# A hybrid decoder layer on one core: TensorE in written order from z through the attention, memory keys and values from one pass over rows of weights, token-major x loaded in halves and again later

## The chip, the core and the metric

The kernel runs on one core of a Trainium2 chip. The metric is device time of one execution, in microseconds (us). Before the change it is 1020.95 us, the median of 3 runs (1020.81 to 1021.11).

## What is computed

One decoder layer on 256 tokens of width 2048, in fp32 (cut to what matters here; SEQ = MEM_LEN = 256):

```python
h = rms_norm(x, g_mix)
z_pool, z_q, z_kv, z_kr, z_mq = split(h @ w_in)          # 512 | 512 | 256 | 64 | 512 columns
y_pool = pool_mixer(z_pool, w_pool, pool_scale)
y_mla  = mla_mixer(z_q, z_kv, z_kr, ...)                 # 8 causal heads, 128 + 64 wide, values 128
y_mem  = memory_cross_attention(z_mq, mem, ...)          # 4 heads of 128
x = x + concat(y_pool, y_mla, y_mem) @ w_o
x = x + conv_glu_ffn(rms_norm(x, g_ffn), ...)            # D_FF = 5632
# memory_cross_attention:
mkv = rms_norm(mem, g_mem) @ w_mem_kv                    # 2048 x 1024: keys 512 | values 512
k = rms_norm(keys per head) ; p = softmax(q k^T / sqrt(128)) ; o = p v
```

## The kernel before

Every large product is made of three fp32r products: weights and activations are each split into a high part (ScalarE copy to fp32r) and a low part (VectorE: value minus high part), and TensorE adds high x high, low x high and high x low. `split_w` (L92) splits 1024 columns of weights at a time into tiles `wh` and `wl`, three buffers each; `load_w` (L82) brings the weights through SyncE's queue into three `wr` buffers. `gemm_t` (L103) gives outputs with features on partitions: per 8 blocks of k, 8 matmuls of 512 columns (L116, `wh`) and 8 of 256 columns (`wl`). `gemm_n` (L121) gives outputs with tokens on partitions: per block of k, token half and output bank three matmuls of the same width (L132, L133, L134). PSUM is two pools of four banks, `psm` and `psa`.

The stages up to the attention, in the order of the program:

- Memory (L283 to L308): `mem_kv(0)` computes the keys in four chunks of 1 MB weights (four blocks of k each), and casts the memory rows `mg` from `memT` on the way (`mem_parts`, L248); `mem_kv(1)` goes over k again for the values, loads the transposed x (`xT_d`, 2 x 1 MB, SyncE's queue), casts it to `xg` (`x_parts`, L259) and finishes the keys (`mem_keys`, L268: scale, head norms, transposes). Sums of squares of the memory go through `SumSq.add` (L200).
- x in token-major form, `x1n` (2 x 1 MB, GpSimd's queue, L336), is loaded once; ScalarE squares it (L341), and later the output projection adds to it.
- mq and rope key (L355 to L375): 16 blocks of k in gemm_n with 288-column matmuls, then row norms and transposes (`to_features`, L226).
- Memory attention: `mem_attn(h)` for 4 heads (L416, L424). `softmax_pv` (L387) does a head's row maxima, exponentials and division, transposes of the weights p (L406), the copy `pT` (L409), the products with the values (L411, L412) and the split of the result (L414).
- z (L437 to L450): six gemm_t of 32 matmuls; then the latent scales (L453 to L462), whose column sums (L217) go over the squares of z.
- The up-projections and the pool branch (L571 to L592), then rope keys (L593 to L604).
- Attention (L633 to L639): `mla(h)` for 8 heads (scores L611 to L614, then `softmax_pv`), and after each head half of one column block of the output projection (`out_part`, L617: 24 matmuls of 512 columns). `out_part(1, ...)` (L662) adds the part over the heads' outputs.

The matmuls of the scores, transposes and values are plain fp32 (a 128- or 256-column product is two instructions; a transpose is one); all others of the list are fp32r. The order on each engine is made by a list scheduler from program order, dependences and its own estimate of times; `keep` (L88) pins an instruction behind the one that was traced before it on its engine. Before the change only a few instructions in this part are kept (L341, L345).

Of the kernel before, what the change touches and what calls it, by code (L numbers as in the profile page):

```python
# [11 lines left out]
F32 = mybir.dt.float32  # L12
# [48 lines left out]
def layer(ctx, tc, xT_d, xn_d, memT_d, vec_d, tab_d, w_z_d, w_mqkr_d, w_q_d, w_kv_d, w_mem_d, w_pool_d, w_o_d,  # L61
# [41 lines left out]
    def gemm_t(ps, raw, o, act, ks, first=True, last=True):  # L103


        ks = list(ks)
        nk = HS // P
        cs = range(0, len(ks), nk)
        for c in cs:
            kc = ks[c:c + nk]  # L110
            hi, lo = split_w(raw, o + c * P, len(kc) * P)

            for low in ((False, True) if c // nk % 2 == 0 else (True, False)):
                for i, k in enumerate(kc):
                    w = (lo if low else hi)[:, i * P:(i + 1) * P]
                    nc.tensor.matmul(ps[:, T if low else 0:2 * T], w, act(k)[:, 0:T] if low else act(k),  # L116
                                     start=first and c + i == 0 and not low,
                                     stop=last and c == cs[-1] and i == len(kc) - 1 and low == (c // nk % 2 == 0),
                                     skip_group_check=True)

    def gemm_n(pss, hi, lo, act, k0, first, last):  # L121
# [4 lines left out]
        for i in range(nk):  # L126
            for tt in range(NT):
                xh = act[:, k0 + i, tt * P:(tt + 1) * P]
                xl = act[:, k0 + i, T + tt * P:T + (tt + 1) * P]
                for j in range(nj):  # L130
                    ps, o = pss[tt][j], slice(j * w, (j + 1) * w)
                    nc.tensor.matmul(ps, xh, hi[:, i, o], start=first and i == 0, stop=False)  # L132
                    nc.tensor.matmul(ps, xl, hi[:, i, o], start=False, stop=False)  # L133
                    nc.tensor.matmul(ps, xh, lo[:, i, o], start=False, stop=last and i == nk - 1)  # L134

    def split_act(dst, src, scale=None):
# [4 lines left out]
        else:  # L141
            nc.scalar.activation(dst[:, 0:T], src, AF.Copy, scale=scale)
            nc.vector.scalar_tensor_tensor(dst[:, T:2 * T], src, scale, dst[:, 0:T].bitcast(F32),
                                           op0=ALU.mult, op1=ALU.subtract)
# [48 lines left out]
    class SumSq:  # L193
# [6 lines left out]
        def add(self, ch):  # L200
            sq = s4()
            nc.scalar.activation(sq[:], ch, AF.Square)
            if self.first:
                nc.vector.tensor_tensor(self.acc[:], sq[:, 0:2, :], sq[:, 2:4, :], op=ALU.add)
            else:
                for h in (0, 2):
                    nc.vector.tensor_tensor(self.acc[:], self.acc[:], sq[:, h:h + 2, :], op=ALU.add)
# [18 lines left out]
    def to_features(dst, src, tt, n, scale=None, eng=None):  # L226

        ps = ps_aux()
# [15 lines left out]
    for a, b in ((0, 1), (1, 2), (2, 4)):  # L244
        nc.sync.dma_start(raw0[:, a * 512:b * 512], w_mem_d[0][:, a * 512:b * 512])
        nc.sync.dma_start(xT[:, a:b, :], memT_d[:, a:b, :])

    def mem_parts(a, b):  # L248
        for j in range(a, b):
            split_act(mg[:, j, :], xT[:, j, :], v("g_mem", j))  # L250
# [8 lines left out]
    def x_parts(a, b):  # L259
        for j in range(a, b):  # L260
            split_act(xg[:, j, :], xT[:, j, :], v("g_mix", j))

    pss_k = []
# [4 lines left out]
    def mem_keys():  # L268
        ps = ps_aux()
        col_sums(ps, ms.done())  # L270
        rsqrt_(rm, ps[:, 0:2], 1.0 / D)
        for tt in range(NT):
            p3 = pss_k[tt][0].rearrange("p (h d) -> p h d", d=XD)
            t = tok()
            t3 = t[:].rearrange("p (h d) -> p h d", d=XD)
            f = fmk[:, tt * XH:(tt + 1) * XH]
            nc.scalar.activation(t3, p3, AF.Copy, scale=rm[:, tt:tt + 1])
            head_sq(f, t3)
            rsqrt_(f, f, 1.0 / XD)
            nc.vector.tensor_tensor(t3, t3, f.unsqueeze(2).to_broadcast([P, XH, XD]), op=ALU.mult)  # L280
            to_features(mkT, t, tt, XH, None, "v")

    def mem_kv(n):  # L283
        pss = [[ps_main()[:]] for _ in range(NT)]
        if n == 0:
            pss_k.extend(pss)
        for c in range(4):
            raw = raw0 if n + c == 0 else load_w(w_mem_d[n * 4 + c], STG, HS if n == 0 else STG)
            if n == 1 and c < 2:
                h = slice(c * 8, c * 8 + 8)  # L290
                nc.sync.dma_start(xT[:, h, :], xT_d[:, h, :])
            if n == 1 and c == 2:
                mem_keys()
            if n == 0 and c < 3:
                nc.sync.dma_start(xT[:, c * 4 + 4:c * 4 + 8, :], memT_d[:, c * 4 + 4:c * 4 + 8, :])
            for i in range(2):
                if n == 0:
                    mem_parts(c * 4 + i * 2, c * 4 + i * 2 + 2)
                elif c > 1:
                    x_parts((c - 2) * 8 + i * 4, (c - 2) * 8 + i * 4 + 4)  # L300
                hi, lo = split_w(raw, i * HS, HS, 512 if n + c == 0 else HS)
                gemm_n(pss, hi[:].rearrange("p (k n) -> p k n", n=512), lo[:].rearrange("p (k n) -> p k n", n=512),
                       mg, c * 4 + i * 2, c + i == 0, c == 3 and i == 1)
            if n == 0:
                ms.add(xT[:, c * 4:(c + 1) * 4, :])
        return pss

    mem_kv(0)  # L308
# [5 lines left out]
    nc.vector.tensor_tensor(gqk[:, 0:1], v("gq_nope"), v("gk_nope"), op=ALU.mult)  # L314
# [625 lines left out]
```

## Time and profile before

| | |
|---|---|
| median of 3 runs | 1020.95 us |
| the profiled execution | 1021.14 us, of which 1019.1 us is the span from first to last instruction |
| TensorE busy | 1013.6 us, 99% |
| VectorE, ScalarE, GpSimd busy | 752.6, 578.8 and 15.3 us |
| granted TensorE clock, mean | 0.999 |
| moved by DMA | 198.06 MB |

Busy time of TensorE is the union of its matmuls, whose ends overlap the next ones' beginnings; what one matmul costs is therefore read from the distance between two starts, not from its duration.

### The profile page before, as it was taken

The page shows a single profiled execution, that of the slowest core. Times are in us where ns is not written, and L with a number is a line of the kernel's source. Part 1 is how long each engine was busy: PE and PEld are TensorE (multiplying, and loading weights), DVE is VectorE, ACT ScalarE, POOL GpSimd, SP SyncE. Part 2 cuts the span into 40 slices and gives each one's busy share as a digit, 9 for nine tenths or more (in the row PEclk, how much of TensorE's full clock was granted, in tenths as well). Part 3 has the DMA queues.
Part 4 walks back from the last instruction along what each step waited for, and adds up shares of the span by engine and source line. Part 5 has one row for each costly group of instructions (what it writes and reads, how often), then busy time and mean ns, then how long its engine had stood idle before and what let it go on. Part 6 is the DMA issues. An engine that isn't in the chain of part 4 may idle for free.

```text
span 1019.1 us, 14119 instructions
## 1 busy us (share of the span) xinstructions
PE 1013.6 (99%) x5356; PEld 867.2 (85%) x5356; DVE 752.6 (74%) x1134; ACT 578.8 (57%) x853; POOL 15.3 (2%) x33
## 2 busy tenths in 40 slices
PE   9999999999999999999999999999999999999998
PEld 7898888877888888888888888888888888888886
DVE  7947689756677777777777776777676788888886
ACT  7657666554566555555555555555555555545653
POOL 0000000000000000000000000000000000010000
PEclk9999999999999999999999999999999999999999
DMA  9765444333665555545455555545555665575551
GB/s 349 289 204 185 160 168 168 132 125 124 226 214 183 205 178 194 192 181 205 167 207 182 190 194 180 205 168 205 186 187 199 256 212 202 206 286 210 206 207 42
DMA packets 30611, 198.06 MB, mean 194 GB/s; under 512 B 3536, under 2 KB 4048, under 8 KB 8656
## 3 DMA queue, kind: packets, MB, share of 16 engines
q1 hardware_dynamic: 28368, 189.44, 52.1%
q0 software_dynamic: 1888, 7.34, 2.0%
q8 instruction: 42, 0.69, 0.3%
q10 hardware_dynamic: 288, 0.38, 0.1%
q14 instruction: 25, 0.20, 0.1%
HBM read 192.96 MB, written 4.19 MB: 193 GB/s over the span
## 4 chain that ended last, share of the span: by engine, by line
PE 98%; DMA 1%; ACT 0%; DVE 0%; SPq 0%; issue 0%
PE psm L116 54%; PE psm L134 6%; PE psm L132 6%; PE psm L133 6%; PE psm L770 4%; PE psa L770 4%; PE psm L768 4%; PE psa L769 4%; PE psa L768 4%; PE psm L769 4%; PE psa L230 1%; PE psa L411 1%; PE psa L406 1%; DMA wr<-in_w_mem 1%; PE psa L611 1%; PE psa L612 1%
## 5 line engine op out<-in xcount | busy, mean ns | idle before, releaser
L99 DVE TENSOR_TENSOR wl<-wr,wh 128x1024 fp32r<-128x1024 f32 (+2 forms) x338 | 392.4, 1165 | 59.0 <-ACT wh L98 53.9
L98 ACT CAST wh<-wr 128x1024 fp32r<-128x1024 f32 (+2 forms) x338 | 339.3, 1006 | 129.3 <-PE psm L133 47.7
L116 PE MATMUL psm<-h,wh 128*128 128x512 f32 x1408 | 337.0, 391 | 0.0
L116 PEld LDWEIGHTS psm<-h,wh 128*128 128x128 f32 x1408 | 258.6, 188 | 49.8
L116 PEld LDWEIGHTS psm<-h,wl 128*128 128x128 f32 x1408 | 180.8, 191 | 7.0
L116 PE MATMUL psm<-h,wl 128*128 128x256 f32 x1408 | 183.0, 283 | 0.0
L99 DVE TENSOR_TENSOR wl<-dn,wh 128x1024 fp32r<-128x1024 f32 x58 | 67.8, 1221 | 26.2 <-ACT wh L98 26.2
L98 ACT CAST wh<-dn 128x1024 fp32r<-128x1024 f32 x58 | 59.2, 1051 | 38.3 <-PE psm L769 21.7
L694 ACT COPY g<-psm 128x256 f32<-128x256 f32 x44 | 16.4, 372 | 91.5 <-PE psm L116 91.5
L695 DVE TENSOR_TENSOR g<-g,psm 128x256 f32<-128x256 f32 x44 | 18.5, 420 | 60.7 <-ACT g L694 60.7
L695 DVE TENSOR_TENSOR u<-u,psm 128x256 f32<-128x256 f32 x44 | 18.5, 422 | 56.2 <-ACT u L694 56.2
L705 ACT ACTIVATE gc<-gc 128x256 f32<-128x256 f32 x44 | 18.4, 418 | 64.0 <-DVE gc L704 64.0
L116 PE MATMUL psm<-xg,wh 128*128 128x512 f32 x160 | 42.7, 402 | 0.0
L704 DVE SCALAR_TENSOR_TENSOR gc<-g,vec,gc 128x255 f32<-128x255 f32 x88 | 42.0, 478 | 0.3
L768 PE MATMUL psa<-wh,aT 128*128 128x512 f32 x104 | 40.5, 389 | 0.0
L770 PE MATMUL psm<-wl,aT 128*128 128x512 f32 x104 | 40.5, 389 | 0.0
L768 PE MATMUL psm<-wh,aT 128*128 128x512 f32 x104 | 40.5, 389 | 0.0
L769 PE MATMUL psa<-wh,aT 128*128 128x512 f32 x104 | 40.5, 389 | 0.0
L769 PE MATMUL psm<-wh,aT 128*128 128x512 f32 x104 | 40.5, 389 | 0.0
L770 PE MATMUL psa<-wl,aT 128*128 128x512 f32 x104 | 40.5, 389 | 0.0
L132 PE MATMUL psm<-wh,cat 128*128 128x512 f32 x96 | 38.5, 401 | 0.0
L134 PE MATMUL psm<-wl,cat 128*128 128x512 f32 x96 | 37.7, 393 | 0.0
(224 smaller groups left out, 1396.8 us busy)
## 6 DMA issues: line engine op xcount, KB each, us to landing
wr<-in_w_g SPq DMA_DIRECT2D x44, 1024.0 KB, 4.8
wr<-in_w_u SPq DMA_DIRECT2D x44, 1024.0 KB, 4.8
wr<-in_w_dn SPq DMA_DIRECT2D x33, 1024.0 KB, 4.8
wr<-in_w_o SPq DMA_DIRECT2D x16, 1024.0 KB, 4.8
dn<-in_w_dn SPq DMA_DIRECT2D x11, 1024.0 KB, 4.8
wr<-in_w_z SPq DMA_DIRECT2D x10, 1024.0 KB, 4.8
wr<-in_w_mqkr SPq DMA_DIRECT2D x8, 576.0 KB, 4.3
wr<-in_w_mem SPq DMA_DIRECT2D x4, 1024.0 KB, 6.5
```

Of the source, the lines that this page charges most:

```text
L98: keep(nc.scalar.copy(hi[:, c:e], raw[:, o + c:o + e]), kept)
L99: keep(nc.vector.tensor_tensor(lo[:, c:e], raw[:, o + c:o + e], hi[:, c:e].bitcast(F32), op=ALU.subtract), kept)
L116: nc.tensor.matmul(ps[:, T if low else 0:2 * T], w, act(k)[:, 0:T] if low else act(k), start=first and c + i == 0 and not low, stop=last a ...
L132: nc.tensor.matmul(ps, xh, hi[:, i, o], start=first and i == 0, stop=False)
L133: nc.tensor.matmul(ps, xl, hi[:, i, o], start=False, stop=False)
L134: nc.tensor.matmul(ps, xh, lo[:, i, o], start=False, stop=last and i == nk - 1)
L695: nc.vector.tensor_tensor(t[:], t[:], ps[:, T:2 * T], op=ALU.add)
L704: nc.vector.scalar_tensor_tensor(gc[:, d:T], g[:, 0:T - d], v(w, f), gc[:, d:T], op0=ALU.mult, op1=ALU.add)
L705: nc.scalar.activation(gc[:], gc[:], AF.Silu)
L768: nc.tensor.matmul(ps, a[0], b[0], start=first, stop=False)
L769: nc.tensor.matmul(ps, a[1], b[0], start=False, stop=False)
L770: nc.tensor.matmul(ps, a[0], b[1], start=False, stop=last)
```

## The change

1. Memory: keys and values in one pass. The weights' rows are packed two blocks of k per 1 MB chunk; per block of k, `gemm_n` writes keys and values of both token halves, in four `psm` banks. Of the first loads, each piece of `memT` goes ahead of the weights. `memT` comes in pieces of two blocks. After every second chunk the four blocks of `memT` just used are squared and replaced by the same blocks of `xT_d`, by four DMAs of 512 KB on GpSimd's queue. `mem_parts`, `split_w`, the squares and `x_parts` are kept in program order on ScalarE and VectorE.
2. mq: its four banks are now `psa`; the memory keys and values are finished beside its first four pieces, the last four `x_parts` after the second. Token-major x comes as four halves of 512 KB through GpSimd's queue into the scratch tile `s4` (two buffers) for the squares alone; `x1n` itself is loaded later, at z's pieces 1 and 3, on SyncE's queue.
3. A class `Head` cuts a head into `score`, `turn` (transposes) and `values`. From z to the end of the first half of the output projection, TensorE's matmuls are kept in written order. In z, a step is written after the first 16 matmuls of each piece (`beside`). In the attention, a step is written after every block of k of `out_part(0, ...)`, six matmuls each (`mla_steps`): rope keys after the 1st, scores of heads 0 and 1 after the 3rd, and from the 6th on, after every 4th, values of head h-1, transposes of head h and scores of head h+2 together.

The diff, cut to its core:

```diff
-    def gemm_t(ps, raw, o, act, ks, first=True, last=True):
+    def gemm_t(ps, raw, o, act, ks, first=True, last=True, kept=False, between=None):
...
+                    keep(nc.tensor.matmul(ps[:, T if low else 0:2 * T], w, ...), kept)
+            if between is not None and c == 0:
+                between()
...
     for a, b in ((0, 1), (1, 2), (2, 4)):
+        nc.sync.dma_start(xT[:, a:b, :], memT_d[:, a:b, :])
         nc.sync.dma_start(raw0[:, a * 512:b * 512], w_mem_d[0][:, a * 512:b * 512])
-        nc.sync.dma_start(xT[:, a:b, :], memT_d[:, a:b, :])
...
-    mem_kv(0)
+    pss = [[ps_main()[:] for _ in range(2)] for _ in range(NT)]
+    for c in range(KD // 2):
+        raw = raw0 if c == 0 else load_w(w_mem_d[c], STG)
+        if 0 < c < KD // 2 - 1:
+            nc.sync.dma_start(xT[:, 2 * c + 2:2 * c + 4, :], memT_d[:, 2 * c + 2:2 * c + 4, :])
+        for i in range(2):
+            k = 2 * c + i
+            mem_parts(k, k + 1)
+            hi, lo = split_w(raw, i * HS, HS, 512 if c == 0 else HS, True)
+            gemm_n(pss, hi[:].unsqueeze(1), lo[:].unsqueeze(1), mg, k, k == 0, k == KD - 1)
+        if c % 2:
+            h = slice(2 * c - 2, 2 * c + 2)
+            ms.add(xT[:, h, :])
+            nc.gpsimd.dma_start(xT[:, h, :], xT_d[:, h, :])
+        if c in (4, 6):
+            x_parts(2 * c - 8, 2 * c - 4)
+    x_parts(8, 12)
...
-    for tt in range(NT):
-        nc.gpsimd.dma_start(x1n[:, tt, :], xn_d[tt])
+    def x_load():
+        i = len(x_pieces)
+        sq = s4()[:].rearrange("p a t -> p (a t)")
+        nc.gpsimd.dma_start(sq, xn_d[i // 2][:, (i % 2) * HS:(i % 2 + 1) * HS])
+        x_pieces.append(sq)
+    def x_square(i):
+        keep(nc.scalar.activation(sq, sq, AF.Square, accum_out=ssq_x[:, i:i + 1]))
...
     for c in range(KD // 2):
         raw = load_w(w_mqkr_d[c], 2 * 576)
...
-        if c in (4, 5):
-            x_squares(c - 4)
+        if c < 2:
+            mem_key(c)
+        elif c < 4:
+            mem_val(c - 2)
+        if c == 1:
+            x_parts(12, 16)
+        for i in {2: (0,), 3: (1,), 5: (2,), 6: (3,)}.get(c, ()):
+            x_square(i)
+        if c < 4:
+            x_load()
...
+    beside = {1: ((0, 0), (1, 0)), 2: ((0, 1),), 3: ((0, 2), (2, 0), (1, 1)), 4: ((1, 2), (3, 0), (2, 1)),
+              5: ((2, 2), (3, 1)), 6: ((3, 2),)}
+    def mem_steps(m):
+        if m == 0:
+            mq_done()
+        for h, step in beside.get(m, ()):
+            (mem_heads[h].score, mem_heads[h].turn, mem_heads[h].values)[step]()
+        if m == 6:
+            latent_scales()
...
     for m in range(6):
         raw = load_w(w_z_d[m], STG)
+        if m in (1, 3):
+            keep(nc.sync.dma_start(x1n[:, m // 2, :], xn_d[m // 2]))
         ps = ps_main()
-        gemm_t(ps, raw, 0, lambda k: xg[:, k, :], range(KD))
+        gemm_t(ps, raw, 0, lambda k: xg[:, k, :], range(KD), kept=True, between=lambda: mem_steps(m))
...
+    def mla_steps():
+        done[0] += 1
+        if done[0] == 1:
+            rope_keys()
+        if done[0] == 3:
+            mla_heads[0].score()
+            mla_heads[1].score()
+        h, r = divmod(done[0] - 6, 4)
+        if r == 0:
+            if 0 < h < H:
+                mla_heads[h - 1].values()
+            if 0 <= h < H:
+                mla_heads[h].turn()
+            if 0 <= h < H - 2:
+                mla_heads[h + 2].score()
+        if done[0] == 4 * H + 4:
+            mla_heads[H - 1].values()
...
-            gemm_n(pss, *w, act, k, c + h == 0, c + h == 2)
+            for r in range(2):
+                kept = i == 0 or n + c == 0
+                gemm_n(pss, *(t[:, r:r + 1] for t in w), act, k + r, c + h + r == 0, c + h + r == 3, kept)
+                if kept:
+                    mla_steps()
```

## Rows read from the trace of the kernel before

**Rows 1.** The page: busy time by engine; the granted clock in 40 slices.
```profile
PE 1013.6 (99%) x5356; PEld 867.2 (85%) x5356; DVE 752.6 (74%) x1134; ACT 578.8 (57%) x853; POOL 15.3 (2%) x33
...
PEclk9999999999999999999999999999999999999999
```

**Rows 2.** Timeline of TensorE in z: start us, us, engine, line, operation, tiles, shape, times.
```profile
116.91 3.82 PE L116 MATMUL psm<-xg,wh 128*128 128x512 f32 x16
120.56 2.08 PE L116 MATMUL psm<-xg,wl 128*128 128x256 f32 x16
122.47 2.01 PE L116 MATMUL psm<-xg,wh 128*128 128x512 f32 x8
```

**Rows 3.** The chain in order of time: start, us, what, times.
```profile
271.67 0.87 PE psa L659 x8
```

**Rows 4.** Waits of TensorE's weight loads: who <- whom: us in total, times, longest.
```profile
PEld psa L411 <- ACT pT L409: 2.6, 9, 0.4
...
PEld psm L134 <- DVE wl L99: 1.0, 3, 0.5
...
PEld psm L133 <- DVE mg L143: 0.7, 2, 0.5
...
PEld psm L132 <- ACT mg L142: 0.6, 1, 0.6
```

**Rows 5.** Timeline of the start: start us, us, engine, line, operation, tiles, [idle before].
```profile
6.62 0.76 PE L132 MATMUL psm<-wh,mg 128*128 128x512 f32 x1
...
8.49 1.14 ACT L98 CAST wh<-wr 128x512 fp32r<-128x512 f32 x2 [1.11 <-DMA wr<-in_w_mem]
...
10.09 0.73 PE L132 MATMUL psm<-wh,mg 128*128 128x512 f32 x2 [0.16 <-ACT mg L142]
```

**Rows 6.** Table by stretches, z and attention: from:to length, busy us (instructions) per engine.
```profile
79.98:124.32 44.34, 44.30 (x249) 37.63 (x248) 31.96 (x78) 29.88 (x63) 0.00 (x0) 1.00 0.41 147
183.05:248.49 65.44, 65.44 (x325) 51.58 (x324) 41.07 (x83) 32.55 (x65) 0.00 (x0) 1.00 0.36 129
```

**Rows 7.** Timeline of TensorE, the transposes of one attention head.
```profile
199.31 0.39 PE L133 MATMUL psm<-wh,cat 128*128 128x512 f32 x1
199.63 0.30 PE L406 MATMUL psa<-identf,p 128*128 128x128 f32 x1
...
200.00 0.38 PE L406 MATMUL psa<-identf,p 128*128 128x128 f32 x2
...
200.47 0.39 PE L133 MATMUL psm<-wh,cat 128*128 128x512 f32 x1
```

**Rows 8.** Timeline: first memory head and first attention head, scores to transposes; z's end.
```profile
82.37 1.21 PE L419 MATMUL psa<-mkT,mqT 128*128 128x256 f32 x4
...
90.64 0.30 PE L406 MATMUL psa<-identf,p 128*128 128x128 f32 x1
...
124.58 0.37 ACT L430 COPY hadd<-psm 128x256 f32<-128x256 f32 x1 [2.32 <-PE psm L116]
...
127.80 0.50 PE L217 MATMUL psa<-ones,zs 128*128 128x1 f32 x4
...
185.71 0.22 PE L614 MATMUL psa<-cmask,identb 128*128 128x128 bf16 x1
...
188.47 1.28 ACT L396 ACT_TABLE_LOAD   x1
...
192.01 0.27 PE L406 MATMUL psa<-identf,p 128*128 128x128 f32 x1
```

**Rows 9.** VectorE to 90 us, groups by line: xcount | busy us, mean ns | idle.
```profile
L99 DVE TENSOR_TENSOR wl<-wr,wh 128x576 fp32r<-128x576 f32 x16 | 11.9, 756 | 13.7 <-ACT wh L98 13.7
...
L143 DVE SCALAR_TENSOR_TENSOR xg<-xT,vec,xg 128x256 fp32r<-128x256 f32 x16 | 6.5, 473 | 0.0
...
L224 DVE TENSOR_REDUCE small<-hsq 128x4 f32<-128x512 f32 x4 | 2.6, 682 | 1.3 <-ACT hsq L223 1.3
```

**Rows 10.** DMA issues from 36 to 60 us: KB each, median us to landing.
```profile
x1n<-in_xn POOLq DMA_DIRECT2D x2, 1024.0 KB, 6.5
```

More of the change, by code (lines that the diff above doesn't have):

```diff
@@ L115, in gemm_t, with gemm_n @@
                     w = (lo if low else hi)[:, i * P:(i + 1) * P]
[L116 to L121, printed above, removed]
+                    keep(nc.tensor.matmul(ps[:, T if low else 0:2 * T], w, act(k)[:, 0:T] if low else act(k),
+                                          start=first and c + i == 0 and not low,
+                                          stop=last and c == cs[-1] and i == len(kc) - 1 and low == (c // nk % 2 == 0),
+                                          skip_group_check=True), kept)
+            if between is not None and c == 0:
+                between()
+    def gemm_n(pss, hi, lo, act, k0, first, last, kept=False):
         nk, n = hi.shape[1], hi.shape[2]
@@ L131, in gemm_n, with split_act @@
                     ps, o = pss[tt][j], slice(j * w, (j + 1) * w)
[L132 to L136, printed above, removed]
+                    keep(nc.tensor.matmul(ps, xh, hi[:, i, o], start=first and i == 0, stop=False), kept)
+                    keep(nc.tensor.matmul(ps, xl, hi[:, i, o], start=False, stop=False), kept)
+                    keep(nc.tensor.matmul(ps, xh, lo[:, i, o], start=False, stop=last and i == nk - 1), kept)
+    def split_act(dst, src, scale=None, kept=False):
         if scale is None:
@@ L283, in mem_kv @@
[L283 to L306, printed above, removed]
@@ L372, in layer @@
-    rsqrt_(fmq, fmq, 1.0 / XD)
-    for tt in range(NT):
-        nc.vector.tensor_scalar(fmq3[:, tt], fmq3[:, tt], rx[:, tt:tt + 1], 1.0 / math.sqrt(XD),
-                                op0=ALU.mult, op1=ALU.mult)
-    rxb = mp.tile([P, T], F32, name="rxb")
-    dx = tok()
-    for tt in range(NT):
-        nc.vector.tensor_scalar(dx[:, tt * P:(tt + 1) * P], identf[:], rx[:, tt:tt + 1], None, op0=ALU.mult)
-    ps = ps_aux()
-    nc.tensor.matmul(ps[:, 0:T], ones[:], dx[:, 0:T], start=True, stop=True)
@@ new lines, in mem_head, with scores @@
+    def mem_head(h):
+        def scores(ps):
+            for tt in range(NT):
+                keep(nc.tensor.matmul(ps[:, tt * M:(tt + 1) * M], mqT[:, h, tt * P:(tt + 1) * P], mkT[:, h, :],
+                                      start=True, stop=True))
+        return Head(scores, ((0, M), (M, 2 * M)), fmq3[:, :, h], lambda k: mv[:, k, h, :], catm[:, h, :])
+    catm = mp.tile([P, XH, 2 * T], F32R, name="catm")
+    mem_heads = [mem_head(h) for h in range(XH)]
+    beside = {1: ((0, 0), (1, 0)), 2: ((0, 1),), 3: ((0, 2), (2, 0), (1, 1)), 4: ((1, 2), (3, 0), (2, 1)),
+              5: ((2, 2), (3, 1)), 6: ((3, 2),)}
@@ L469, in pool_in @@
         ps = ps_main()
-        gemm_t(ps, raw, 0, lambda k: xg[:, k, :], range(KD))
+        gemm_t(ps, raw, 0, lambda k: xg[:, k, :], range(KD), kept=g == 0, between=lambda: mem_steps(6 + g))
         half_add(zp[:, g, :], ps)
@@ new lines, in mla_head, with scores @@
+    def mla_head(h):
+        def scores(ps):
+            for tt, (a, n) in enumerate(((0, P), (P, 2 * P))):
+                q = slice(tt * P, (tt + 1) * P)
+                for l, r, o, b, e in ((qnT[:, h, q], knT[:, h, 0:n], a, True, False),
+                                      (qrT[:, h // 2, q], krT[:, h, 0:n], a, False, False),
+                                      (identb[:], cmask[:], a + n - P, False, True)):
+                    keep(nc.tensor.matmul(ps[:, o:a + n], l, r, start=b, stop=e, skip_group_check=True))
+        return Head(scores, ((0, P), (P, 3 * P)), fq3[:, :, h], lambda k: vv[:, k, h, :], cat[:, 4 + h, :])
@@ new lines, in layer @@
+    mla_heads = [mla_head(h) for h in range(H)]
+    done = [0]
+    def mla_steps():
[15 more added lines that the diff above has]
+            mla_heads[H - 1].values()
```

236 lines of the change are left out of this document (116 added, 120 removed).

## The prediction

> **What bounds the kernel now.** I read the page's busy times first. TensorE is busy for 1013.6 of 1019.1 us at the full of its two clock levels [rows 1], so the change, which removes no matmul, can only gain what TensorE loses between matmuls. That is invisible in busy time, because a late matmul's record is merely longer. So I read distances between starts. In z, 16 matmuls of 512 columns take 3.65 us and 16 of 256 columns 1.91 us [rows 2], 0.228 and 0.119 us each; eight fp32 transposes take 0.87 us [rows 3], 0.109 each. For an fp32 instruction of 256 columns I take twice that, 0.218, for the small bf16 mask product half, 0.055 (estimates by columns). A stretch's length minus the sum of its instructions at these paces is what TensorE loses there.
>
> z, from 79.98 to 124.32 us: 96 + 96 matmuls (21.9 + 11.4 us), four transposes and one product of mq's end (0.9), and four memory heads of eight 256-column instructions and four transposes (2.18 each, 8.7) make 42.9 of 44.34 us [rows 6]. Lost: 1.4 us. The attention, 183.05 to 248.49 us, holds 325 instructions [rows 6], two of them tails of earlier ones; 136 are the heads' (per head 3 transposes, 4 of values, 10 of scores: 0.33 + 0.65 + 1.42 = 2.40 us, 19.2 in all), 187 are fp32r (42.6). That is 61.8 of 65.44 us. Lost: 3.6 us.
>
> Where it is lost is seen in a head's transposes [rows 7]: from the matmul at 199.31 to the one at 200.47 there are three matmuls and three transposes, 0.68 + 0.33 = 1.01 us, yet 1.16 pass. The scheduler put one transpose, a matmul, and then the other two: every passage from fp32r to fp32 and back costs. The timeline has 14 such fp32 groups in the z stretch (0.10 us each) and 28 in the attention (0.13 each). Part of it is TensorE waiting for pT, 2.6 us over nine weight loads [rows 4].
>
> The third place is the start. The first real matmul starts at 6.62 us, and by 18 us the weight loads have waited for the low parts `wl` (1.0), for `mg` from VectorE (0.7) and from ScalarE (0.6) [rows 4]; the distances between starts in that stretch, 46 matmuls, sum to 2.1 us over pace. The waiting is at the casts: ScalarE first waits 1.11 us for weights until 8.49, then casts memory rows, and TensorE resumes at 10.09 [rows 5]. Per 24 matmuls (5.5 us at pace) the first pass over the memory has two weight tiles, four memory blocks and one square of four blocks to cast; after the change there are two blocks and half a square.
>
> **The change, part by part.** Its sum is made against 1021.14 us, of which 2.0 lie outside the span; the median is 0.2 lower, so I take the difference off the median.
>
> *Start and memory.* 192 matmuls stay 192. Bytes needed by the second and third weight tile are the same (1.5 and 2.5 MB), but `memT` now precedes the weights, so the second half of the first chunk lands after 0.25 MB more, about 0.6 us later than 8.49. Walking the queues: first matmul about 6.7 (memory cast, then weight cast, instead of the other way), second tile at about 9.8 instead of 10.09, third at about 12.8, each with 0.2 to 0.3 us lost; after that the cast engines are ahead. I put 0.9 us lost instead of 2.1: **-1.2 us** (bounds -1.8 and 0).
>
> *z.* Eight groups instead of 14 (the end of mq as before, then one per piece): at 0.10 us, **-0.6 us** (bounds -1.4, all of it, and 0).
>
> *Attention.* Ten groups instead of 28: scores of two heads, eight slots, the last values. At 0.13 that leaves 1.3 us; a group with scores also has the mask product inside, so I add 0.5 for eight scores. 3.6 - 1.8: **-1.8 us** (bounds -2.8 and -0.6). The seven slots' values find pT ready since a whole slot, 24 matmuls, so the 2.6 us of waits for pT are in this gain and not counted again.
>
> *What the written order makes TensorE wait for.* TensorE takes matmuls in that order, so behind a transposed p that is not ready all of z or of the output projection stands still. Each first user, with its cover:
> - Memory head 0: scores to transposes took 90.64 - 83.58 = 7.1 us before [rows 8], with head norms and the table load of the exponential in it. The cover now is the other scores (0.87) and 32 matmuls of z (5.55): 6.4 us. The norms will be done earlier: 0.2 us (0 to 1.0). Later heads have 6.9 us or more.
> - Column sums of z: z's last piece was read from 124.58 and its sum came at 127.80, 3.2 us [rows 8]; the cover is 16 matmuls and four value products, 3.6 us: 0.1 (0 to 0.7).
> - Rope keys: four VectorE copies of some 0.7 us (the 512-wide reduction is the nearest row) [rows 9] under 12 matmuls and the first products: 0.2 (0 to 0.8).
> - Attention head 0: scores end at 185.77, first transpose at 192.01, 6.2 us, with a 1.28 us table load in it [rows 8]. The cover is the scores of head 1 (1.4) and 18 matmuls (4.1): 5.5 us. 0.5 (0 to 1.9). The other heads have two slots, some 15 us; the last values 12 matmuls for one copy, nothing.
> Together **+1.0 us**, bounds 0 and 4.4.
>
> *mq.* Its matmuls and their width stay. Beside its first two pieces VectorE now gets: rotation tables (16 small ones, moved by the keep behind the memory's scale), keys' norms and copies (six 512-wide of 0.68), and eight `x_parts` of 0.47 [rows 9], some 10 us with the six weight splits of 0.76, against 6.4 us of TensorE's work plus a lead of two tiles. Splits aren't kept here, so they can slip in while the key chain waits for TensorE and ScalarE: **+0.2 us** (bounds 0 and 5).
>
> *DMAs.* Token-major x is read twice: 2 MB more. In z the queue is SyncE's, where two 1 MB loads stand between weights; the DMA engines are 41% busy there [rows 6], so nothing. In mq the four halves go through GpSimd's queue behind the last transposed block; a 1 MB load took 6.5 us to land on it [rows 10]. The first square stands two pieces (6.4 us) after its load, the last two three pieces after the square that frees their buffer: nothing, but see the rivals. ScalarE's queue holds the weight casts behind each square.
>
> On that queue the Trainium skill speaks against the change: SBUF — State Buffer, section "SBUF: two separate sides", says that loads issued from GpSimd can't get their descriptors written while VectorE runs an operation in a two-port mode. The 6.5 us were measured with VectorE working on fp32 all along, and no row shows a starved load. By the rule the late-load rival below would come up; by the row it doesn't, and the sum stays.
>
> Sum: -1.2 - 0.6 - 1.8 + 1.0 + 0.2 = -2.4 us. **Forecast 1018.5 us.**
>
> **The rivals.** (A) *The waits eat the gain.* The covers of the two first heads miss by 1 us each, the column sums and rope keys by 0.5, and mq by 0.5: -3.6 + 3.5 gives 1020.8; with half of them 1019.1. For it: covers of 6.4 and 5.5 us stand against 7.1 and 6.2 measured. Against it: those contain waiting behind casts that the scheduler put in.
> (B) *The loss sits in each fp32 instruction, not in the group.* Then grouping gives nothing, only the start gains: 1020.95 - 1.2 + 1.2 = 1021.0. Against it: eight transposes in a row run at 0.109 [rows 3].
> (C) *Everything is ready.* No new waits, gains near their bounds, -1.5 - 0.8 - 2.4: 1016.2.
> (D) *Slower: the head of mq.* ScalarE and VectorE stand at the last four `x_parts` and at the first squares, which are kept, until GpSimd's loads land; behind them wait the splits of mq's next pieces, and TensorE after two tiles (3.2 us). With a square 6.5 us late per pair, two pairs, less the leads, plus VectorE's 5 us crowd, TensorE stands 6 to 8 us: about 1024.5 to 1026.5. It decides from about 4.5 us of standing on (2.4 of gain plus 2.0). For it: 10 us of VectorE's work against 6.4. Against it: the loads are issued one or two pieces ahead.
>
> **How the numbers follow.** A measurement can tell about 0.2%, 2 us, from no change: faster means below 1018.9, slower above 1023.0. Forecast 0.50 (its own range 1016.9 to 1019.4), A 0.20, B 0.10, C 0.12, D 0.08. Faster: C and four fifths of the forecast's range, 0.52; slower: D, 0.08; the same: 0.40. The range takes C's centre and A's far end: 1015.9 to 1021.2 leaves out part of C and D, about 0.15.
>
> **What the profile after would show.** Right: in the attention one fp32 group per 24 matmuls, values, transposes and scores of three heads side by side, and a stretch of 136 head instructions and 192 matmuls in some 64.8 us instead of 66.6; in z groups only after 16 matmuls; third weight tile of the memory at about 12.8 us. Wrong: weight loads of TensorE that wait over 0.5 us for p or pT (A), a long wait of mq's first product for `wl` or of ScalarE for a DMA into `s` or `xT` (D), or fp32 groups whose instructions lie as far apart as before (B). Casts that fall behind in a written stretch would show as TensorE waiting for `wh` or `wl` in the attention; I expect none, with VectorE busy 41 of 65 us there [rows 6].

## The result and the profile after

The changed kernel takes **1015.86 us** (median of 4 runs, 1015.66 to 1016.01) against 1021.03 us of the kernel before on the same chip (4 runs): a ratio of 0.9947, 95% interval 0.993 to 0.9964. It is 5.2 us faster where 2.4 were forecast, and 0.04 us below the low end of the range. What happened is nearly rival C, "Everything is ready" (1016.2).

The page of the kernel after, busy time by engine: TensorE has 5356 instructions as before [rows 1] and is still busy for 99% of a span that is 5.2 us shorter.

```profile
span 1013.9 us, 14132 instructions
...
PE 1008.2 (99%) x5356; PEld 868.6 (86%) x5356; DVE 752.4 (74%) x1134; ACT 577.5 (57%) x853; POOL 18.5 (2%) x39
```

The table by stretches, the same two stages as in [rows 6], each from its first to its last start (length, busy us and instructions of PE, PEld, DVE, ACT, POOL, then clock, DMA share, GB/s):

```profile
77.98:120.46 42.48, 42.48 (x248) 37.61 (x247) 32.03 (x79) 30.63 (x66) 0.00 (x0) 1.00 0.58 209
179.16:249.82 70.66, 70.66 (x362) 59.28 (x360) 45.41 (x90) 35.01 (x70) 0.00 (x0) 1.00 0.40 137
```

A busy time equal to the length says nothing by itself, as before; the distances between starts do. I sum them here at slightly finer paces, all from rows further down or counted in the same way in both traces: 0.227 us for 512 fp32r columns, 0.1195 for 256, 0.215 for an fp32 instruction of 256 columns, 0.109 for one of 128, 0.055 for a mask product. By these, z lost 1.6 us before and the attention 3.9.

- z after: 96 x 0.227 + 96 x 0.1195 + 30 fp32 instructions of 256 columns x 0.215 + 24 of 128 x 0.109 = 42.33 us in a stretch of 42.48. **Lost: 0.15 us.**
- Attention after: 216 output products (49.03), 8 heads of 2.38 (19.05), eight transposes of the rope keys (0.87) = 68.95 of 70.66. **Lost: 1.7 us.**

Timeline of TensorE in z, around the first memory head and one later piece (start us, us, engine, line, operation, tiles, shape, times):

```profile
87.64 1.89 PE L438 MATMUL psa<-mkT,mqT 128*128 128x256 f32 x8
89.18 1.30 PE L116 MATMUL psm<-xg,wl 128*128 128x256 f32 x8
90.32 3.82 PE L116 MATMUL psm<-xg,wh 128*128 128x512 f32 x16
93.97 1.12 PE L116 MATMUL psm<-xg,wl 128*128 128x256 f32 x8
94.93 0.60 PE L421 MATMUL psa<-identf,p 128*128 128x128 f32 x4
```

The stretch of 16 wide matmuls and two times eight narrow ones is unbroken between one fp32 group and the next, and from the last narrow matmul into the transposes at 94.93 no time is lost. Here is why: VectorE's rows of the division that makes p (L415) for that head, and for the first head of the attention:

```profile
92.07 0.62 DVE L415 TENSOR_SCALAR p<-p,st 128x256 f32<-128x256 f32 x2
...
190.04 0.55 DVE L415 TENSOR_SCALAR p<-p,st 128x128 f32<-128x128 f32 x2
```

The first p is there at 92.69, 2.2 us ahead of its transposes; the attention's first at 190.59, 0.8 us ahead of 191.41. One slot of the attention, and the matmuls behind it:

```profile
198.82 0.59 PE L429 MATMUL psa<-pT,qkv 128*128 128x256 f32 x2
199.25 0.38 PE L431 MATMUL psa<-pT,qkv 128*128 128x128 f32 x2
199.47 0.49 PE L421 MATMUL psa<-identf,p 128*128 128x128 f32 x3
199.80 0.39 PE L653 MATMUL psa<-qkv 128*128 128x128 f32 x2
200.02 0.39 PE L653 MATMUL psa<-qkv,mqT 128*128 128x128 f32 x2
200.25 0.22 PE L653 MATMUL psa<-cmask,identb 128*128 128x128 bf16 x1
...
201.22 0.22 PE L653 MATMUL psa<-cmask,identb 128*128 128x128 bf16 x1
201.25 0.48 PE L134 MATMUL psm<-wh,cat 128*128 128x512 f32 x1
201.56 0.40 PE L135 MATMUL psm<-wh,cat 128*128 128x512 f32 x1
```

Values of one head, transposes of the next, scores of the one after stand side by side: two values take 0.43 us (198.82 to 199.25, the pace of 0.215), three transposes 0.33. Only at the mask does something stick out: 201.22 to 201.56 is 0.34 us for a mask product and one wide matmul that together should take 0.28.

Last, the waits of TensorE's weight loads from 77 to 250 us (engine, line, waited for: us in total, times, longest); all but the third line are transposes of the up-projection stage:

```profile
PEld psa L232 <- DVE tok L604: 0.5, 2, 0.3
PEld psa L232 <- DVE tok L549: 0.3, 1, 0.3
PEld psa L527 <- PE psm L136: 0.3, 1, 0.3
PEld psa L232 <- issue: 0.2, 1, 0.2
PEld psa L232 <- ACT tok L562: 0.2, 1, 0.2
```

The wait for `pT` that heads [rows 4] (2.6 us) is gone, and none for p has come.

The budget of the 5.2 us:

| | forecast | traces |
|---|---|---|
| z, and waits in it | -0.6 + 0.3 | -1.4 |
| attention, and waits in it | -1.8 + 0.7 | -2.2 |
| start, memory, mq | -1.2 + 0.2 | -1.0 |
| outside the span (2.0 us before, 1015.66 - 1013.9 = 1.8 after) | 0 | -0.2 |

The third line is from z's first start: on average 78.2 us in eleven executions with the new memory stage (77.8 to 78.7) against 79.6 in two of the kernel before (79.98 and 79.30); of the 1.4 us, 0.4 are four transposes of mq's end that now come after that start. The lines add up to 4.8; the median of the kernel before moves by 0.4 us from one set of runs to the next (1020.84 to 1021.24), which covers the rest.

### The profile page after: what moved, and what is told of

Same layout as the page of the kernel before. It is cut to its first block, busy times and chain, and to the rows that moved or that the text cites. A ratio compares the mean times of both kernels' runs of the same rounds, so it can differ in the third digit from the quotient of the medians.

```text
span 1013.9 us, 14132 instructions
## 1 busy us (share of the span) xinstructions
PE 1008.2 (99%) x5356; PEld 868.6 (86%) x5356; DVE 752.4 (74%) x1134; ACT 577.5 (57%) x853; POOL 18.5 (2%) x39
## 4 chain that ended last, share of the span: by engine, by line
PE 99%; DMA 0%; SPq 0%; DVE 0%; ACT 0%; issue 0%
PE psm L116 54%; PE psm L134 5%; PE psm L136 5%; PE psm L135 5%; PE psm L834 4%; PE psa L834 4%; PE psm L833 4%; PE psa L832 4%; PE psa L833 4%; PE psm L832 4%; PE psa L653 1%; PE psa L134 1%; PE psa L136 1%; PE psa L135 1%; PE psa L232 1%; PE psa L429 1%
## 5 line engine op out<-in xcount | busy, mean ns | idle before, releaser
L99 DVE TENSOR_TENSOR wl<-wr,wh 128x1024 fp32r<-128x1024 f32 (+2 forms) x338 | 392.4, 1165 | 65.4 <-ACT wh L98 59.7
L99 DVE TENSOR_TENSOR wl<-dn,wh 128x1024 fp32r<-128x1024 f32 x58 | 67.8, 1221 | 26.3 <-ACT wh L98 26.3
L759 DVE TENSOR_TENSOR g<-g,psm 128x256 f32<-128x256 f32 x44 | 18.5, 420 | 61.0 <-ACT g L758 61.0
L759 DVE TENSOR_TENSOR u<-u,psm 128x256 f32<-128x256 f32 x44 | 18.5, 421 | 55.6 <-ACT u L758 55.6
L769 ACT ACTIVATE gc<-gc 128x256 f32<-128x256 f32 x44 | 18.4, 418 | 63.8 <-DVE gc L768 63.7
L116 PE MATMUL psm<-xg,wh 128*128 128x512 f32 x160 | 40.0, 394 | 0.0
```

Source lines behind the costliest of these rows:

```text
L99: keep(nc.vector.tensor_tensor(lo[:, c:e], raw[:, o + c:o + e], hi[:, c:e].bitcast(F32), op=ALU.subtract), kept)
L116: keep(nc.tensor.matmul(ps[:, T if low else 0:2 * T], w, act(k)[:, 0:T] if low else act(k), start=first and c + i == 0 and not low, stop=l ...
L759: nc.vector.tensor_tensor(t[:], t[:], ps[:, T:2 * T], op=ALU.add)
L769: nc.scalar.activation(gc[:], gc[:], AF.Silu)
```

## The experiments

Each is the changed kernel with one edit. "Against before" is the median less that of the kernel before in the same set of runs (7 to 11 runs); the changed kernel's own is -5.17.

| run | median, us | against before | ratio, 95% interval | lost in z, attention |
|---|---|---|---|---|
| groups apart | 1016.02 | -5.22 | 0.9947 [0.9932, 0.9961] | 0.15, 1.86 |
| no masks | 1014.24 | -7.00 | 0.993 [0.9914, 0.9947] | 0.15, 0.85 |
| masks last | 1015.61 | -5.63 | 0.9942 [0.9927, 0.9957] | 0.15, 1.25 |
| old memory stage | 1017.60 | -3.64 | 0.9968 [0.9956, 0.9979] | 0.16, 1.71 |
| late scores | 1016.63 | -4.57 | 0.9958 [0.9943, 0.9973] | 0.15, 2.97 |
| attention's order free | 1016.53 | -4.67 | 0.9955 [0.9939, 0.9972] | 0.15, 1.71 |
| z's order free | 1015.63 | -5.57 | 0.9947 [0.9932, 0.9962] | 0.15, 1.71 |
| weights first | 1015.72 | -5.48 | 0.9947 [0.9933, 0.9962] | 0.15, 1.69 |
| whole heads | 1018.03 | -2.81 | 0.9977 [0.9966, 0.9988] | 0.15, 3.98 |
| masks side by side | 1015.52 | -5.32 | 0.9947 [0.9933, 0.996] | 0.15, 1.37 |

The questions: is it the number of fp32 groups that cost (the prediction's price of 0.10 to 0.13 us each), or that their operands weren't ready? What do the waits, the written order and the memory stage add? And what is the 1.7 us that the attention still loses?

**Groups apart.** Values, transposes and scores of a slot are put behind different blocks of k, so the attention has 23 fp32 groups instead of 11.

```diff
-        if r == 0:
-            if 0 < h < H:
-                mla_heads[h - 1].values()
-            if 0 <= h < H:
-                mla_heads[h].turn()
-            if 0 <= h < H - 2:
-                mla_heads[h + 2].score()
+        if r == 0 and 0 < h < H:
+            mla_heads[h - 1].values()
+        if r == (1 if h < H - 1 else 0) and 0 <= h < H:
+            mla_heads[h].turn()
+        if r == 2 and 0 <= h < H - 2:
+            mla_heads[h + 2].score()
```

> The changed kernel with the steps of a slot apart in the attention: values of head h-1, transposes of head h and scores of head h+2 follow different blocks of k, six matmuls between them. 12 fp32 groups more, every operand still ready long before. Theory R (a group costs nothing when what it loads is ready): the attention loses at most 0.3 us more, 1015.9 to 1016.2. Theory G, that of the prediction (each passage into fp32 and back costs 0.10 to 0.13 us): 12 groups cost 1.2 to 1.6 us more, 1017.1 to 1017.5.

Timeline of TensorE in this run, one group of values and one of transposes alone between fp32r matmuls:

```profile
199.33 0.59 PE L429 MATMUL psa<-pT,qkv 128*128 128x256 f32 x2
199.76 0.38 PE L431 MATMUL psa<-pT,qkv 128*128 128x128 f32 x2
199.90 0.48 PE L134 MATMUL psm<-wh,cat 128*128 128x512 f32 x1
200.22 0.39 PE L135 MATMUL psm<-wh,cat 128*128 128x512 f32 x1
...
201.14 0.40 PE L136 MATMUL psm<-wl,cat 128*128 128x512 f32 x1
201.38 0.49 PE L421 MATMUL psa<-identf,p 128*128 128x128 f32 x3
201.62 0.48 PE L134 MATMUL psm<-wh,cat 128*128 128x512 f32 x1
```

From 199.33 to 200.22 lie four fp32 instructions and one matmul: 0.89 us, where 2 x 0.215 + 2 x 0.109 + 0.227 = 0.875. (The record of the first fp32r matmul behind a group starts early; the next start shows the distance.) Twelve more groups cost 1.86 - 1.71 = 0.15 us, 0.012 each. The price per group falls: a group whose operands are there is nearly free.

**Whole heads.** The reverse: scores, transposes and values of a head are traced together, ahead of the head's half of the output projection, as before; the order of the attention is the scheduler's (diff cut).

```diff
         for c in range(2):
+            if n + c == 0:
+                rope_keys()
+            head = mla_heads[2 * n + c]
+            head.score()
+            head.turn()
+            head.values()
             out_part(0, n, pss, c)
```

> The attention's order is left to the scheduler again, and the scores, the transposes and the values of a head stand together in the program, ahead of the head's half of the output projection, as they did before; the keys' rope too. All else is the changed kernel's. Theory R (cutting a head into steps that stand far apart in the program makes the operands ready, and the order by hand adds nothing): the attention again loses about 3.9 us over the pace of its instructions instead of 1.7, the head's groups of fp32 instructions double to 28, and the time is 1015.9 + 2.2 = 1018.1. Rival S (the attention's gain comes from elsewhere, from an x that no longer occupies GpSimd's loads or from tiles that come free earlier): the loss stays at 1.7 and the time at 1015.9.

The attention loses 3.98 us (3.94 before the change), in 29 groups with the rope keys' (28 before), and the time rises by 2.2 us over the changed kernel's (1018.03 - 1015.86), as theory R has it. The weight loads' waits in this run's attention, 179 to 246 us:

```profile
PEld psa L430 <- ACT pT L425: 2.2, 7, 0.4
PEld psa L422 <- PE psm L136: 1.1, 3, 0.4
PEld psa L422 <- issue: 0.8, 3, 0.3
PEld psa L422 <- PE psm L135: 0.4, 1, 0.4
PEld psa L654 <- DVE qkv L644: 0.3, 1, 0.3
```

The three rows of L422 are transposes. The profile names TensorE or nothing as what ended their waits, but p had only just come: in seven of the eight heads the first transpose starts 0.14 to 0.21 us behind the first half of p, and in seven of eight the first product with the values 0.05 to 0.06 us behind the copy `pT`. The changed kernel has no row at all in that table. So cutting the heads is what gains in the attention, by having operands ready. No run put whole heads back into z: that its gain has the same cause is read from the waits there (below).

**The order left free.** In the attention, and in another run in z, the matmuls lose their `keep`, while the steps stay where they are in the program (of the first run, cut):

```diff
-                    keep(nc.tensor.matmul(ps[:, o:a + n], l, r, start=b, stop=e, skip_group_check=True))
+                    nc.tensor.matmul(ps[:, o:a + n], l, r, start=b, stop=e, skip_group_check=True)
...
-                gemm_n(pss, *(t[:, r:r + 1] for t in w), act, k + r, c + h + r == 0, c + h + r == 3, kept)
+                gemm_n(pss, *(t[:, r:r + 1] for t in w), act, k + r, c + h + r == 0, c + h + r == 3, False)
```

> The changed kernel with the order of TensorE in the attention left to the scheduler again; the heads stay cut into steps, traced in the same places. If the written order itself makes the groups ready: the loss of before comes back, 2.0 to 2.3 us, 1018.0. If it is the cutting of heads into steps far apart: 0 to 0.5 us, 1015.9 to 1016.4.

> The changed kernel with the order of TensorE in z left to the scheduler; the memory heads stay cut into steps in the same places. If the written order is what counts: 1.0 to 1.4 us slower, 1017.1. If the steps far apart are enough: 0 to 0.3, 1016.0.

Losses and numbers of groups are those of the changed kernel to 0.01 us in both. The first run's four executions, 1016.19 to 1016.86, still lie above all four of the changed kernel (1015.66 to 1016.01). In the one that was profiled (1016.34) the excess is at the start: it lost 2.21 us over the first 46 memory matmuls (1.26 in the changed kernel's). The other three have no trace, so what raises them is not shown. In z and the attention the written order adds nothing that can be measured: what counts is where the steps stand in the program.

**Late scores.** The scores of heads 0 and 1 come two blocks of k later, which leaves six matmuls between them and the first transposes.

```diff
-        if done[0] == 3:
+        if done[0] == 5:
             mla_heads[0].score()
```

> The changed kernel with the scores of attention heads 0 and 1 two blocks of k later (after the 5th instead of the 3rd), so that only 6 matmuls and the scores of head 1 cover the softmax of head 0. In the changed kernel p of head 0 was ready at 190.59 us and its first transpose started at 191.41: 0.8 us to spare. Theory R: 12 matmuls less cover is 2.7 us, so TensorE stands 1.9 us at the first transpose: 1017.8. By the chain as the prediction read it from before (6.2 us): it would stand 3.4 us, 1019.3. If the written order does not make TensorE wait: 1015.9.

Timeline of TensorE in this run, the first transposes, with the idle time ahead of them:

```profile
189.68 0.22 PE L653 MATMUL psa<-cmask,identb 128*128 128x128 bf16 x1
192.36 0.61 PE L421 MATMUL psa<-identf,p 128*128 128x128 f32 x3 [1.01 <-DVE p L415]
```

The attention loses 1.26 us more; the profiled execution is 1.1 us longer than the changed kernel's (its start was 0.2 us quicker), the median 0.8. So TensorE does stand when the cover is too short, but from the end of head 0's scores (188.20) to its transposes 4.2 us pass, not the 6.2 of before; in the changed kernel it was 185.64 to 190.59, 4.9, with two 1.2 us weight splits in VectorE's queue. The chain is shorter than the cover of 5.5 us on which the prediction put 0.5 us of standing.

**The masks.** One run leaves the causal mask's products out (so p is not masked), another puts both of a head at the end of its scores (this order of accumulation does not give the kernel's sums; like the first, the run serves for its time alone).

```diff
-                                      (qrT[:, h // 2, q], krT[:, h, 0:n], a, False, False),
-                                      (identb[:], cmask[:], a + n - P, False, True)):
+                                      (qrT[:, h // 2, q], krT[:, h, 0:n], a, False, True)):
```

> The changed kernel without the bf16 mask product of the scores (the causal mask is left out). Theory R: the 0.13 us that a slot still loses belong to the two passages from bf16 to fp32 and fp32r in it; with the 16 products (0.055 us each at pace, 0.9) go 8 x 0.12 = 1.0 us of loss: 1.8 to 1.9 us faster, 1014.0. Theory G: only the products' own 0.9 us: 1015.0, and each group still loses 0.13.

> The changed kernel with both mask products of a head at the end of its scores, side by side, instead of one in the middle and one at the end. Theory R: one passage from bf16 fewer per head, 8 x 0.06 us: 1015.4. Theory G: the groups are the same, nothing: 1015.9.

Without the 16 products the attention loses 0.85 us instead of 1.71, beyond the products' own 0.88: 16 passages to bf16 and back at 0.054 us each. With both products side by side half of the passages fall away, and the loss falls by 0.46. The 0.85 us that are left lie in no one place: they come to 2.5 ns on each of some 340 starts. Whether that is a pace taken too short or a small loss at each start the rows don't tell.

**Masks side by side, and weights first.** In the same spirit, with the sums intact: the second half of a head begins with its mask product. This run also loads the first weights ahead of the memory rows, which was tried alone too.

```diff
...
+                prods = [(qnT[:, h, q], knT[:, h, 0:n], a), (qrT[:, h // 2, q], krT[:, h, 0:n], a)]
+                prods.insert(0 if tt else 2, (identb[:], cmask[:], a + n - P))
+                for i, (l, r, o) in enumerate(prods):
+                    keep(nc.tensor.matmul(ps[:, o:a + n], l, r, start=i == 0, stop=i == 2, skip_group_check=True))
```

> In each of the attention's heads the second half's mask product is the first of that half instead of the last, so that the two bf16 products of a head stand side by side and two passages between bf16 and fp32 fall away; the first loads of the memory stage have the weights ahead of the rows. If the passages cost about 0.06 us each, as the run without masks says, the attention loses 1.71 - 8 x 0.06 = 1.25 and the time is 1015.9 - 0.5 = 1015.4. Rival: what costs is the bf16 product itself and its first accumulation, not the passage; then the loss stays at 1.7 and the time at 1015.9. The order of the first loads is expected to give under 0.3 either way.

> The changed kernel with the weights ahead of the memory rows in the first three pairs of loads, as before. In the changed kernel ScalarE waits for the weights at 5.10, 6.96 and 8.96 us; if these landings set the start, weights first gains 0.2 to 0.5 us: 1015.5. If the memory rows' cast then ends last: 0 to 0.4 us slower, 1016.2.

Timeline of the run with the masks side by side, one slot:

```profile
199.95 0.39 PE L653 MATMUL psa<-qkv,mqT 128*128 128x128 f32 x2
200.17 0.28 PE L653 MATMUL psa<-cmask,identb 128*128 128x128 bf16 x2
200.28 0.65 PE L653 MATMUL psa<-qkv 128*128 128x256 f32 x2
```

The attention loses 1.37 us instead of 1.71: 0.34 gained where 0.5 were expected. In time, 1015.52 (1015.21 to 1016.49) stands beside 1015.86 and, in the same set of runs, 1015.85 for the changed kernel: too little to tell apart. The order of the first loads makes no difference either.

**The old memory stage**, in the changed kernel: two passes over the memory, weights ahead of rows, nothing kept there; the values' and keys' ends where they were (the edit undoes part 1 of the change and the steps beside mq).

> The changed kernel with the memory stage of the kernel before (keys first, then values, weights ahead of memory rows, casts not kept, keys finished inside the second pass). By the two traces the stage is worth 2.0 us up to z's first matmul, of which 0.5 is an earlier first matmul: 1017.7 to 1017.9. If the earlier first matmul is the chance of one execution and not the new order: 1017.3 to 1017.4. By the prediction's own term (1.2 less 0.2): 1016.9.

The median rises by 1.7 us. The run's profiled execution (1019.8 us) lost 4.4 us over the first 46 memory matmuls and is the longest of its six; the other five took 1017.29 to 1018.32. Its rows tell why (timeline of TensorE; then the table by stretches):

```profile
11.28 0.74 PE L134 MATMUL psm<-wh,mg 128*128 128x512 f32 x2 [1.67 <-ACT mg L144]
...
12.61:16.02 3.41, 3.41 (x9) 2.65 (x8) 3.15 (x6) 3.41 (x7) 0.00 (x0) 0.50 1.03 417
16.02:19.43 3.41, 3.41 (x16) 2.79 (x15) 3.38 (x6) 3.41 (x7) 0.00 (x0) 1.00 1.02 406
```

TensorE stood 1.67 us for the memory rows, and soon after, from 12.61 to 16.02 us, its granted clock was 0.50, the lower of its two levels. Eight matmuls there stand 0.43 us apart instead of 0.227, which costs 1.6 us. The standing and the low clock make 3.4 of the 4.4 us, and no other trace here shows such a fall at the start, so this execution doesn't size the stage.

**Both kernels once more, unchanged**, for the start.

> The kernel before, unchanged, profiled once more, to see how much of the 1.7 us at the start lies in the start of the one execution that was profiled. Theory M (the new memory stage is what gains): first matmul near 6.6, 46th memory matmul near 19.2, that is over a microsecond later than the 17.6 to 18.5 of the kernels with the new stage. Rival V (chance in the start): the 46th memory matmul falls within 17.6 to 18.5.

> The changed kernel, unchanged, profiled once more, beside the kernel before: first matmul at 5.5 to 6.6, 46th memory matmul at 17.6 to 18.5, losses of 0.15 in z and 1.7 in the attention if these are the kernel's own and not the execution's.

Timeline of TensorE, the starts of the second and third tile's matmuls in this second profile of the kernel before, where [rows 5] had 10.09:

```profile
9.61 0.62 PE L132 MATMUL psm<-wh,mg 128*128 128x512 f32 x2
...
12.93 0.50 PE L132 MATMUL psm<-wh,mg 128*128 128x512 f32 x1
```

The 46th memory matmul (counted from nought, so 46 stand ahead of it) starts at 19.19 and 18.54 us in the two profiles of before, and at 17.80 and 17.99 in those of the changed kernel; over eleven executions with the new stage it is 17.6 to 18.5. The losses in z (1.59 and 1.55 before, 0.15 and 0.15 after) and in the attention (3.93 and 3.94, 1.71 and 1.71) repeat to 0.04 us. Neither theory M nor rival V is borne out: the second 46th matmul of before, at 18.54, is not over a microsecond later than the eleven, and not within their range either. Both starts of before come later than all eleven, but the difference, 0.6 to 1.4 us, is about the size of the start's own scatter, 0.9.

## Why the prediction was off, step by step

**Right: where the time was.** The losses in z, attention and start that distances between starts showed are the three places where the time came from, and each gained. The second reading of the parts that weren't touched agrees: from z's end to the attention 1.47 us were lost before and 1.45 after (a column sum's product counted at its 0.112 us). Two sums of [rows 4] are of the whole execution and were booked for one stage: by 18 us the waits for `wl` are 0.8, not 1.0, and in the attention those for `pT` are 2.2, not 2.6. Neither enters the forecast.

**Wrong: the price of a group that remains.** "Eight groups instead of 14: at 0.10 us" and "Ten groups instead of 28. At 0.13 that leaves 1.3 us" took the whole loss as a price per passage between fp32r and fp32, so that what stays of groups had to keep its share. The run with groups apart puts that price at 0.012 us. The 0.10 to 0.13 were TensorE standing in front of a transpose or product whose p or pT wasn't there. Three lines of the kernel before show it: VectorE's division that makes p and ScalarE's copy `pT` for the head of [rows 7], and the transposes' wait for p in z (the list of [rows 4]):

```profile
199.21 0.55 DVE L400 TENSOR_SCALAR p<-p,st 128x128 f32<-128x128 f32 x2
...
200.42 0.48 ACT L409 COPY pT<-psa 128x384 f32<-128x384 f32 x1 [0.96 <-PE psa L406]
...
PEld psa L406 <- DVE p L400: 1.0, 3, 0.4
```

The first half of p is there at 199.49 and the first transpose starts at 199.63; the second half comes at 199.75 and the next transposes start at 200.00; the copy ends at 200.90 and the products with the values start at 200.96. The scheduler's one transpose, a matmul and two transposes was TensorE taking p as it came. In seven of the eight heads the first transpose starts 0.14 to 0.20 us behind the first half of p, and in z's four 0.05 to 0.15; in the changed kernel it is 1.1 us or more in every head. The prediction had part of the evidence in its hands, `pT` at 2.6 us in [rows 4], but booked it as part of the groups' price instead of as its cause. Rival B ("in each fp32 instruction") falls by the same row. In z the whole loss went, -1.4 instead of -0.6, which was the bound of that step. In the attention 1.7 stay, and they are not the ten groups' price: half is the mask's passages, for which 0.5 had been added, half the 2.5 ns on each start. The two terms together were to gain 2.4 us and gained 3.6.

**Wrong: the waits of the written order, +1.0.** None appeared, so the other 1.0 of the miss is here. Memory head 0: 2.2 us to spare where 0.2 were to be missing. Attention head 0: 0.8 to spare where 0.5 were put. The step that failed is the use of before's distances from scores to transposes, 7.1 and 6.2 us [rows 8], as lengths of the chains. They are upper bounds: in the kernel before, three weight splits of 1.22 us (L99) stand on VectorE between head 0's scores and its p in the attention, two of them inside the softmax; in z two splits and work on the norms and the rope key do. The prediction names this as the argument against rival A and still kept half of it in the sum. That the term's mechanism exists is shown by the late scores, +1.26 us with a cover of six matmuls. Column sums: the eight products follow the last value product without a gap, at 0.11 us each (from 124.09). Rope keys: no wait is listed.

**Right in sum: start and memory -1.2, mq +0.2.** The third weight tile was to start at about 12.8; it starts at 12.81, and the second at 10.09 instead of 9.8. The timeline of the start after:

```profile
6.09 0.48 PE L134 MATMUL psm<-wh,mg 128*128 128x512 f32 x1
6.41 0.39 PE L135 MATMUL psm<-wh,mg 128*128 128x512 f32 x1
...
7.63 0.50 PE L134 MATMUL psm<-wh,mg 128*128 128x512 f32 x1 [0.60 <-ACT wh L98]
...
12.81 0.39 PE L134 MATMUL psm<-wh,mg 128*128 128x512 f32 x1
```

TensorE starts sooner, at 6.09 instead of 6.62 (its clock rose sooner, last section), then stands 0.6 us for the second half of the first weights, and from 8.7 on it doesn't wait again before mq. From the 46th memory matmul to z 0.19 us are lost instead of 0.35: the matmuls beside mq's crowd lost 0.32 instead of 0.17, so the +0.2 was right, though the list behind it adds up to 12.4 us on VectorE by its own rows and not "some 10"; the rest of the memory stage gave 0.3. By the traces the sum of these steps is the forecast -1.0; by the run with the old stage it is -1.5 to -1.7. Which of the two is nearer stays open, since the start of one execution scatters by as much as they differ; a single profile's 2.1 us of loss at the start, on which the term rested, was 1.5 in the second.

**Right: DMAs 0, and rival D didn't come.** DMA issues from 36 to 80 us (KB each, median us to landing):

```profile
s<-in_xn POOLq DMA_DIRECT2D x4, 512.0 KB, 5.2
x1n<-in_xn SPq DMA_DIRECT2D x2, 1024.0 KB, 8.6
xT<-in_xT POOLq DMA_DIRECT2D x1, 512.0 KB, 5.5
```

The same up to 36 us:

```profile
xT<-in_memT SPq DMA_DIRECT2D x7, 256.0 KB, 8.5
xT<-in_xT POOLq DMA_DIRECT2D x3, 512.0 KB, 8.3
```

From 36 us on the loads through GpSimd's queue land in 5.2 and 5.5 us, while VectorE works through the crowd beside mq; the 6.5 of [rows 10] were for twice the bytes. The three transposed loads in the memory stage took 8.3, but SyncE's smaller loads beside them took 8.5. The starving that the Trainium skill (SBUF — State Buffer, "SBUF: two separate sides") warns of for such loads doesn't show here either. That is no test of the rule: no row tells whether VectorE's instructions beside these loads ran in a two-port mode. The 8.6 us of `x1n` on SyncE's queue cost nothing, as z's stretch shows.

**The share given to C.** With the price of a ready group at zero and no waits, the steps alone give -1.2 - 1.4 - 2.2 + 0.2 = -4.6, about 1016.3. That is C, which the prediction held at 0.12 as if its parts had to reach their ends independently; z and the attention got there together, since they had one cause.

## What to carry to other kernels

Before a loss at small instructions is priced per group, look whether each stands behind a late operand; a cheap test is to count groups that are surely ready and read their distance. A distance between producer and consumer in the kernel before is an upper bound on a chain, and so is no evidence that a shorter cover will be missed. To have operands ready, trace the steps of a chain far apart in the program, one unit of other work between them; an order by hand on top of it gave nothing here.

## What the runs showed that had not been expected

- A passage between fp32r and fp32 costs about 0.012 us per group when the operands are there, but one to bf16 and back about 0.054 us per product (attention without masks). Putting two bf16 products side by side took back 0.34 to 0.46 us of 0.86.
- The start scatters: in eleven executions with the new memory stage the first real matmul starts anywhere from 5.5 to 6.65 us (the order of the first loads differs in two of them) and the 46th from 17.6 to 18.5, so a term below 1 us at the start can't be sized from one profile of each kernel. Part of it is TensorE's clock. Ahead of the first real matmul stand 26 warm-up matmuls. They start 0.213 us apart at first and 0.111 later, and where the change falls among them it comes where the trace's record of the granted clock begins, with its full level; ahead of that the tables print 1.00 with no record behind it. Twice the distance is what the granted 0.50 made of the wide matmuls in the run with the old memory stage, so the start of each execution reads as the lower level. In the nine executions with the memory rows first the record begins at 4.1 to 6.9 us, and the first real matmul follows it: 5.53 us where it begins at 4.13, 6.62 where it begins at 6.91. By the 46th nothing is left of that (18.4 and 17.9 in these two). In the two profiles of the kernel before it begins at 7.23 and 6.82, after the start of the first real matmul, which stands 0.57 and 0.41 us ahead of the second (6.62 to 7.19, 6.62 to 7.03), where 0.23 is the later pace. The Trainium skill (TensorE: Matmul & The Clock Gate, Part 1) says that how many matmuls of a kernel run at the low clock differs from run to run; the traces agree.
- The time outside the span fell from 2.0 us (in each of 27 runs of the kernel before, within 0.1) to 1.8 in all kernels with the change, the one with the old memory stage too. No row here shows what it is.
